# Attention's values: four heads' sums in one PSUM bank, three narrow products in place of two, and a third bank for the maxima

## The chip, the cores and the metric

The kernel runs on one core of a Trainium2 chip. The metric is device time in microseconds (us), lower is better. Before the change it is 2776.42 us, the median of three runs (2773.62 to 2778.46).

A core has five engines that run side by side, each with its own queue of instructions in a fixed order: TensorE (PE in the profile, its weight loads PEld), VectorE (DVE), ScalarE (ACT), GpSimd (POOL), and SyncE (SP), which issues the DMAs. TensorE writes its products to PSUM, where the kernel's tiles have up to 512 f32 columns on 128 partitions, each tile a bank of its own; VectorE and ScalarE read them there.

## The reference, cut to what matters

One layer of a transformer with two mixers beside each other: 2048 tokens of width 1024 and 256 context tokens. A modulated RMS norm and an input projection give the queries, keys and values of a bidirectional retention (4 heads of 128) and of an attention (8 heads of 64 in 2 groups of 4 heads, each group with one key and value head). Behind them come the output projection, a second norm, a feed-forward part of width 4096 with a squared ReLU, and a last norm. The change touches attention alone:

```python
s = jnp.einsum('bqkgd,bskd->bkgqs', q, k).astype(jnp.float32) * ATT_SCALE
p = jax.nn.softmax(s, axis=-1).astype(v.dtype)
return jnp.einsum('bkgqs,bskd->bqkgd', p, v)
```

All of it is f32: 2304 keys for each query, a softmax over them, and the weighted sum of the values.

## The kernel before, in words

The kernel has three stretches: input projections and what they need (to about 640 us), attention together with retention and the output projection (640 to 1560 us), and the feed-forward part with the last norm (from there to the end).

To keep the precision of f32 with f16 products, operands are split into a high part (the value rounded to f16) and a low part (the rest, in f16 as well). A sum of products then has three parts: high by high, low by high, and high by low.

Attention is cut into 32 groups: a block of 128 queries (`t`) and a key and value head (`g`) with its four query heads. The class `Group` (L147 to L261) holds the steps of one group. For a group:

- `piece` (L167) forms scores of 128 queries with 512 keys, with the high parts of the queries alone, in a PSUM bank with the tag `mp` (L172; L176 for the last 256 keys of two heads at once). `maximum` (L178) reduces each to its largest value with VectorE (L185). There are 18 pieces. `least` (L187) joins them into the tile `mt` (L191), `turn` (L193) transposes `mt` with TensorE into one more bank of the tag `mp` (L196), and `rows` (L198, ScalarE, L199) and `rows2` (L201, VectorE, L203) read it there, to add the negative maximum as rows to the queries `qr`.
- `scores` (L205) forms, for a tile of 128 keys, the scores of the four heads with two products of 512 columns (L209, L210) in a bank with the tag `st`. `exp` (L212, L215) writes the exponentials with ScalarE to `p`, `cast` (L217, L219) their high parts `phi`, and `low` (L221) their low parts `plo`, on GpSimd for two key tiles at once (L226) or on VectorE for one (L228).
- `values` (L230) multiplies them with the values. The tile `wv` holds for each key the 64 high parts of the value, a column of ones (so that the sum of the exponentials comes out as a 65th column), and the 64 low parts: 129 columns. For each of two key tiles and four heads there are two products: `plo` with the first 65 columns (L242), and `phi` with all 129 (L243). The sum for high times low thus has 64 columns of its own. Two heads take 258 columns, so the four heads take two banks, `o0` and `o1`. Each bank is begun, over all its columns, with a product of a tile of zeros (L234, `start=True`), and all others add to that (`start=False`).
- `evacuate` (L245) copies both banks to `so` with ScalarE (L247, L248), `invert` (L250) takes the reciprocal of the 65th column with VectorE, and `combine` (L254) adds the two sums with GpSimd (L260) and multiplies them with the reciprocal (L261).

The pools of PSUM in this stretch are `psS` (two banks each for `mp` and `st`), `psV` (one for each of `o0` and `o1`) and `psX` (two banks for retention and the output projection): eight in all. A tile of a tag takes a free place of that tag, and its first writer waits until the readers of the tile that was there are done.

The order of all instructions is set by the program: a counter `k` runs over steps, 18 for a group, and every step calls the functions that were registered for it, in the order of the phases begin, scores, piece, maximum, early, exp, cast, low, chain, pe, values, late, dma. `attention` (L1290) registers a group's 18 pieces in steps k to k + 17, each maximum one step later, `least` in step k + 18, `turn` in step k + 19 ahead of that step's piece, `rows` in k + 20 and `rows2` in k + 21. So the first pieces of a group stand around the turn of the group before it. A group's scores follow 22 steps after its first piece, and every second step holds a burst of `values`, 288 bursts in all (9 in each of 32 groups). Each engine works off its instructions in this order. The group 0 takes its maxima earlier, beside the projections.

Of the kernel before, what the change touches and what calls it, by code (L numbers as in the profile page):

```python
# [11 lines left out]
F32 = mybir.dt.float32  # L12
F32R = mybir.dt.float32r
F16 = mybir.dt.float16
BF16 = mybir.dt.bfloat16
I32 = mybir.dt.int32
AF = mybir.ActivationFunctionType
ALU = mybir.AluOpType
# [4 lines left out]
P = 128  # L23
# [6 lines left out]
NK = NT + NC  # L30
H = 4
CH = 128
HD = 64
# [4 lines left out]
EARLY = 1  # L38

ROW = 8192.0  # L40
VW = 2 * HD + 1
POOL_PAIRS = (0, 2, 4, 6, 7)

C_RQ, C_RK, C_RV, C_RG, C_AQ, C_AKV = 0, 512, 1024, 1536, 2048, 2560
# [6 lines left out]
def bc(ap, shape):  # L51
    return ap.to_broadcast(shape)
# [3 lines left out]
def layer_kernel(ctx: ExitStack, tc: tile.TileContext, a: dict, out: bass.AP):  # L56
    nc = tc.nc
    mm = nc.tensor.matmul
# [75 lines left out]
    kp = keep.enter_context(tc.tile_pool(name="kp", bufs=1, reuse_waits="tile"))  # L134
# [2 lines left out]
    ks = kp.tile([P, 2, NK * P], F16, name="ks")  # L137


    wv = kp.tile([P, 2, NK, VW + 1], F16, name="wv")  # L140
    inv = kp.tile([P, 1], F32, name="inv")

    dT, tf, tb = (kp.tile([P, 4, P], F32, name=n) for n in ("dT", "tf", "tb"))
# [3 lines left out]
    class Group:  # L147
# [16 lines left out]
            tag = f"nm{self.n}" if self.n < EARLY else "nm"  # L164
            self.nm = pool.tile([P, 2, 2, 5], F32, name="nm", tag=tag)

        def piece(self, i, pool=None, tag="mp"):  # L167
            m = self.m[i] = (pool or psS).tile([P, 512], F32, name="mp", tag=tag)
            h, r = i // 9 * 2, i % 9
            if r < 8:  # L170
                k = ks[:, self.g, r % 4 * 512 : (r % 4 + 1) * 512]
                mm(m, self.qr[:, 0, h + r // 4], k, start=True, stop=True)  # L172
            else:
                for e in range(2):
                    k = ks[:, self.g, 2048:]
                    mm(m[:, 256 * e : 256 * e + 256], self.qr[:, 0, h + e], k, start=True, stop=True)  # L176
# [14 lines left out]
                nc.vector.tensor_reduce(mt[:, :, c], nm, axis=AX.X, op=ALU.min)  # L191

        def turn(self):  # L193
            self.m = psS.tile([P, 4, P], F32, name="mp", tag="mp")
            for h in range(4):
                nc.tensor.transpose(self.m[:, h], self.mt[:, h], ident)  # L196

# [31 lines left out]

        def values(self, j):  # L230
            if j == 0:
                self.o = [psV.tile([P, 2, VW], F32, name=f"o{b}", tag=f"o{b}") for b in range(2)]
                for o in self.o:
                    mm(o, zeros, wv[:, 0, :2, :VW], start=True, stop=False)  # L234
            hi, lo = self.hi.pop(j), self.lo.pop(j)
            for i in range(2):
                v = wv[:, self.g, 2 * j + i]
                for h in range(4):
                    o = self.o[h // 2][:, h % 2]
                    c = slice(h * P, (h + 1) * P)  # L240
                    last = 2 * j + i == NK - 1 and h % 2 == 1
                    mm(o[:, : HD + 1], lo[:, i, c], v[:, : HD + 1], start=False, stop=False)  # L242
                    mm(o, hi[:, i, c], v[:, :VW], start=False, stop=last)  # L243

        def evacuate(self):  # L245
            self.so = op.tile([P, 4, VW], F32, name="so", tag="so")
            nc.scalar.activation(self.so[:, :2], self.o[0], AF.Copy)  # L247
            nc.scalar.activation(self.so[:, 2:], self.o[1], AF.Copy)  # L248

        def invert(self):  # L250
            self.r = sm.tile([P, 4], F32, name="r", tag="r")
# [2 lines left out]
        def combine(self, ats):  # L254

            if self.g == 0:
                ats[self.t] = room_tile("ma")
            at = ats[self.t][:, 4 * HD * self.g : 4 * HD * (self.g + 1)]
            at = at.rearrange("p (h d) -> p h d", h=4)
            nc.gpsimd.tensor_tensor(at, self.so[:, :, :HD], self.so[:, :, HD + 1 :], op=ALU.add)  # L260
            nc.gpsimd.tensor_tensor(at, at, bc(self.r.unsqueeze(2), [P, 4, HD]), op=ALU.mult)  # L261

    order = [(t, g) for t in range(NT - 1, -1, -1) for g in range(2)]
    groups = [Group(n, *o) for n, o in enumerate(order)]
# [2 lines left out]
    with ExitStack() as st:  # L267
# [5 lines left out]
        op = st.enter_context(tc.tile_pool(name="op", bufs=2, reuse_waits="tile"))  # L273
# [20 lines left out]
        def at(q, step, fn, *args):  # L294
            plan.setdefault((q, step), []).append((fn, args))
# [466 lines left out]
        def value_parts(q0):  # L762

            x = {}

            def load():
                nc.vector.memset(wv[:, :, :, HD : HD + 1], 1.0)
                for i in range(3):
                    x[i] = xp.tile([P, 2, 6, HD], F32, name="vn", tag="x")
                    nc.sync.dma_start(x[i], av_d[:, :, 6 * i : 6 * i + 6])  # L770
                w = xp.tile([P, P + 8], F32, name="vma", tag="x")
                x["m"], x["r"], x["s"], x["e"] = w[:, :P], w[:, P : P + 4], w[:, P + 4 : P + 5], w[:, P + 5 : P + 6]

            def greatest(i):
                v = x[i].rearrange("p g k d -> p (g k d)")
                nc.vector.tensor_reduce(
                    x["r"][:, i : i + 1], v, axis=AX.X, op=ALU.max, apply_absolute_value=True
                )
                if i == 2:
                    nc.vector.tensor_reduce(x["r"][:, 3:], x["r"][:, :3], axis=AX.X, op=ALU.max)  # L780

            def write():
                nc.sync.dma_start(vm_d, x["r"][:, 3:])

            def read():
                nc.sync.dma_start(x["m"], vm_d.partition_broadcast(P))

            def scale():
                e = x["e"]
                nc.vector.tensor_reduce(e, x["m"], axis=AX.X, op=ALU.max)  # L790
                nc.vector.tensor_scalar_max(e, e, 1e-30)
                nc.vector.tensor_single_scalar(e.bitcast(I32), e.bitcast(I32), 0x7F800000, op=ALU.bitwise_and)
                nc.vector.reciprocal(x["s"], e)
                nc.vector.tensor_scalar_mul(x["s"], x["s"], 8192.0)
                nc.vector.tensor_scalar_mul(inv, e, 2.0**-13)

            def parts(i):
                w, v = wv[:, :, 6 * i : 6 * i + 6], x[i]
                nc.vector.tensor_scalar_mul(v, v, x["s"])
                nc.scalar.activation(w[:, :, :, :HD], v, AF.Copy)  # L800
                nc.vector.tensor_tensor(w[:, :, :, HD + 1 : VW], v, w[:, :, :, :HD], op=ALU.subtract)

            at(q0, "dma", load)
            for i in range(3):
                at(q0 + 3 + i, "extra", greatest, i)
                at(q0 + 11 + i, "extra", parts, i)
            at(q0 + 5, "store", write)
            at(q0 + 7, "store", read)
            at(q0 + 10, "extra", scale)
# [340 lines left out]
        first = weights[0]  # L1150
# [74 lines left out]
    op = pool(attn, "op2", 2)  # L1225
    qp = pool(attn, "qp")
    vp = pool(attn, "vp")
    psS = pool(attn, "psS", 2, space=PSUM)
    psV = pool(attn, "psV", space=PSUM)
# [9 lines left out]
    nc.vector.tensor_tensor(unit, ident[:, 64:65], ident[:, 96:97], op=ALU.add)  # L1239
    nc.vector.tensor_tensor(unit, unit, ident[:, 80:81], op=ALU.add)  # L1240
    nc.vector.tensor_scalar_mul(unit, unit, ROW)
    zeros = vp.tile([P, P], F16, name="zeros")
    nc.vector.memset(zeros, 0.0)
    mts = [vp.tile([P, 4, P], F32, name=f"mt{i}") for i in range(2)]
    for mt in mts:
        nc.gpsimd.memset(mt, 0.0)
# [13 lines left out]
    def on(k, phase, fn, *args):  # L1260
        events.setdefault((k, phase), []).append((fn, args))
# [28 lines left out]
    def attention():  # L1290
        for n, g in enumerate(groups):
            k = NK * n
            if n > 0:
                on(k - 14 if n >= EARLY else k + NK - 6, "dma", g.load)
            else:
                on(k + NK, "begin", g.load)
            if n >= EARLY:
                on(k - 1, "late", g.minima, sm)
                for i in range(NK):
                    on(k + i, "piece", g.piece, i)  # L1300
                    on(k + i + 1, "maximum", g.maximum, i)
            on(k + NK, "chain", g.least, mts[n % 2])
            on(k + NK + 1, "piece", g.turn)
            on(k + NK + 2, "cast", g.rows)
            on(k + NK + 3, "early", g.rows2)
            k += LAG
            for i in range(NK):
                on(k + i, "scores", g.scores, i)
                on(k + i + 1, "exp", g.exp, i)
            for j in range(NK // 2):  # L1310
                on(k + 2 * j + 3, "cast", g.cast, j)
                if j in POOL_PAIRS:
                    on(k + 2 * j + 4, "low", g.low, j)
                else:
                    for i in range(2):
                        on(k + 2 * j + 4 + i, "low", g.low, j, i)
                on(k + 2 * j + 6, "values", g.values, j)
            k += NK + 5
            on(k, "cast", g.evacuate)
            on(k + 1, "chain", g.invert)  # L1320
            on(k + 2, "late", g.combine, ats)
        return NK * len(groups) + LAG + 8
# [311 lines left out]
    for n, t in enumerate(range(NT - 1, -1, -1)):  # L1634
        made_at, last = output_tile(t, R0 + 43 + RF * n, n == NT - 1)
# [362 lines left out]
    with tc.manual_schedule():  # L1998
# [8 lines left out]
        for b in range(2 * NB):  # L2007
            g = 7 * b
# [51 lines left out]
        g = NU * NS  # L2060
# [15 lines left out]
        for lo, g0 in ((0, g + 10), (4, g + 14)):  # L2076
# [3 lines left out]
            for m in range(lo, lo + 4):  # L2080
                k = g0 + 1 + m % 4 // 2
# [3 lines left out]
        g = NU * (2 * NS - 1)  # L2085
# [5 lines left out]
        for g in range(4, NU * 2 * NS):  # L2091
            b, n = divmod(g, 7)
# [26 lines left out]
        lo, hi = slice(0, HALF), slice(HALF, D)  # L2119
# [91 lines left out]
```

## Time and profile before

| | |
|---|---|
| time, median of three runs | 2776.42 us (2773.62 to 2778.46) |
| the profiled execution: its span, from the first to the last instruction (what lies around it isn't given) | 2774.9 us |
| TensorE's mean granted clock | 0.989 of full speed |
| MATMULs and LDWEIGHTS in it | 16896 each |
| products of `values` | 2304 of 65 columns, 2304 of 129 columns, 64 of zeros |

The profile is of one execution. The busy time of an engine is the time in which one of its instructions runs. Matmuls are pipelined: the next one starts while the one before is still on its way through the array, so that a row's length (0.38 us for 512 columns) is longer than the distance to the next start (0.22 us), and what a product costs a busy TensorE is the latter. Idle time in front of an instruction stands in brackets or behind the bar, with what ended it. Weight loads (LDWEIGHTS, PEld) run beside the products.

### The profile page before, as it was taken

The numbers are of one execution on the slowest core, as the hardware profiler recorded it, in microseconds if no ns is written. First come the engines' busy times: TensorE is split into PE (matmuls) and PEld (weight loads), VectorE is DVE, ScalarE is ACT, GpSimd is POOL, SyncE is SP. The second block draws the span as 40 slices with busy tenths as digits, with TensorE's granted clock in tenths as the row PEclk, the third lists the DMA queues.
The fourth block names the chain that finished last, engine by engine and source line by source line (L and its number), as shares of the span: only waits on it lengthen the run. The fifth ranks groups of instructions, "written<-read, shape, count | busy, mean of one in ns | idle before, by whom it ended". The sixth has DMA issues, their size and how long they took to land.

```text
span 2774.9 us, 45229 instructions
## 1 busy us (share of the span) xinstructions
PE 2657.9 (96%) x16896; PEld 1432.6 (52%) x16896; DVE 2103.3 (76%) x3306; ACT 1600.3 (58%) x2736; POOL 1423.2 (51%) x1182
## 2 busy tenths in 40 slices
PE   7999999888999999999999889999999999999998
PEld 2545654445666666666666544444444444444443
DVE  5857677668877777777777577989999956666676
ACT  3633762227877777787778576555554564434442
POOL 2623772365755657676667644454556721111155
PEclk9999999999999999999999999999999999999999
DMA  7478758584111231322222665665657332222223
GB/s 265 132 251 294 225 167 271 150 265 169 48 60 53 67 96 57 98 79 86 86 76 83 239 209 175 204 190 179 200 187 273 129 108 83 84 89 79 84 76 137
DMA packets 275045, 402.51 MB, mean 145 GB/s; under 512 B 107717, under 2 KB 163141, under 8 KB 272522
## 3 DMA queue, kind: packets, MB, share of 16 engines
q1 hardware_dynamic: 271802, 394.90, 43.9%
q10 hardware_dynamic: 3024, 4.72, 0.5%
q8 instruction: 133, 2.18, 0.3%
q14 instruction: 86, 0.70, 0.1%
HBM read 294.54 MB, written 105.00 MB: 144 GB/s over the span
## 4 chain that ended last, share of the span: by engine, by line
PE 76%; DVE 11%; DMA 4%; issue 3%; ACT 3%; POOL 2%; SPq 0%; POOLq 0%; ACTq 0%; DVEq 0%
PE pd L1894 6%; PE pd L1892 6%; PE pd L1893 6%; PE pu L1715 6%; PE pu L1717 6%; PE pu L1716 6%; PE pso L650 5%; PE pso L651 5%; PE pso L652 5%; PE o L243 3%; PE st L209 3%; PE st L210 3%; PE mp L172 3%; DVE plo L228 2%; DVE nm L185 2%
## 5 line engine op out<-in xcount | busy, mean ns | idle before, releaser
L185 DVE TENSOR_REDUCE nm<-mp 128x1 f32<-128x512 f32 (+1 forms) x576 | 390.3, 685 | 158.6 <-PE mp L172 131.4
L215 ACT ACTIVATE p<-st 128x512 f32<-128x512 f32 x576 | 339.1, 599 | 178.1 <-PE st L210 122.5
L226 POOL TENSOR_TENSOR plo<-p,phi 128x1024 f16<-128x1024 f32 x160 | 351.4, 2197 | 173.2 <-ACT phi L219 141.7
L1715 PE MATMUL pu<-hf,w1f 128*128 128x512 f16 x896 | 341.0, 381 | 7.2 <-ACT w L1732 3.8
L1717 PE MATMUL pu<-hf,w1f 128*128 128x512 f16 x896 | 341.0, 381 | 0.0
L1716 PE MATMUL pu<-hf,w1f 128*128 128x512 f16 x896 | 340.7, 380 | 0.0
L219 ACT ACTIVATE phi<-p 128x1024 f16<-128x1024 f32 x288 | 304.1, 1056 | 0.0
L651 PE MATMUL pso<-wlo,h 128*128 128x512 f16 (+1 forms) x816 | 296.2, 363 | 2.0 <-DVE wlo L548 2.0
L650 PE MATMUL pso<-whi,h 128*128 128x512 f16 (+1 forms) x816 | 296.5, 363 | 1.3 <-ACT whi L547 1.3
L652 PE MATMUL pso<-whi,h 128*128 128x512 f16 (+1 forms) x816 | 296.0, 363 | 0.0
L228 DVE TENSOR_TENSOR plo<-p,phi 128x512 f16<-128x512 f32 x256 | 235.1, 919 | 16.1 <-ACT phi L219 14.9
L242 PE MATMUL o<-wv,plo 128*128 128x65 f16 x2304 | 234.9, 193 | 13.0 <-POOL plo L226 6.6
L243 PE MATMUL o<-wv,phi 128*128 128x129 f16 x2304 | 242.7, 220 | 0.0
L242 PEld LDWEIGHTS <-plo 128*128 128x128 f16 x2304 | 206.1, 98 | 55.6 <-POOL plo L226 15.9
L1918 DVE SCALAR_TENSOR_TENSOR acc<-pd,scv,acc 128x512 f32<-128x512 f32 x248 | 183.1, 743 | 54.0 <-PE pd L1894 51.4
L209 PE MATMUL st<-qr,ks 128*128 128x512 f16 x576 | 219.6, 381 | 4.4 <-ACT p L215 3.8
L210 PE MATMUL st<-qr,ks 128*128 128x512 f16 x576 | 219.7, 381 | 0.1
L243 PEld LDWEIGHTS <-phi 128*128 128x128 f16 x2304 | 205.2, 97 | 21.3 <-issue 0.5
L172 PE MATMUL mp<-ks,qr 128*128 128x512 f16 x512 | 196.1, 383 | 17.2 <-DVE nm L185 17.0
L1680 POOL TENSOR_TENSOR w1s<-w1r 128x512 f32<-128x512 f32 x64 | 92.4, 1444 | 233.4 <-ACT w L1754 159.9
L1892 PE MATMUL pd<-w2t,us 128*128 128x512 f16 x496 | 188.0, 379 | 1.7 <-DVE acc L1918 1.7
L1893 PE MATMUL pd<-w2t,us 128*128 128x512 f16 x496 | 188.0, 379 | 0.0
(377 smaller groups left out, 6109.2 us busy)
## 6 DMA issues: line engine op xcount, KB each, us to landing
w2t<-w2f SPq DMA_DIRECT2D x98, 512.0 KB, 4.2
wm<-in_w_ff SPq DMA_DIRECT2D x64, 512.0 KB, 5.0
w1r<-in_w_ff SPq DMA_DIRECT2D x64, 512.0 KB, 4.7
w2f<-w2f SPq DMA_DIRECT2D x98, 256.0 KB, 2.4
wmr<-in_w_mod SPq DMA_DIRECT2D x32, 512.0 KB, 5.3
w2r<-in_w_ff SPq DMA_DIRECT2D x32, 512.0 KB, 4.2
hf<-hp SPq DMA_DIRECT2D x56, 256.0 KB, 3.5
hf<-hf SPq DMA_DIRECT2D x14, 1024.0 KB, 7.2
```

What stands on the lines that cost most here:

```text
L185: nc.vector.tensor_reduce(dst, src, axis=AX.X, op=ALU.max, negate=True)
L226: nc.gpsimd.tensor_tensor(lo, p, hi, op=ALU.subtract)
L242: mm(o[:, : HD + 1], lo[:, i, c], v[:, : HD + 1], start=False, stop=False)
L243: mm(o, hi[:, i, c], v[:, :VW], start=False, stop=last)
L650: mm(self.ps[:, c], hi[:, k], wh, start=k == 0, stop=False)
L651: mm(self.ps[:, c], hi[:, k], wl, start=False, stop=False)
L652: mm(self.ps[:, c], lo[:, k], wh, start=False, stop=k == KT - 1)
L1715: mm(pu[c], whi, hi, start=first and k == 0, stop=False, **more)
L1716: mm(pu[c], whi, lo, start=False, stop=False, **more)
L1717: mm(pu[c], wlo, hi, start=False, stop=k == 3, **more)
L1892: mm(ps, uh, wh, start=first and j == 0, stop=False, **more)
L1893: mm(ps, uh, wl, start=False, stop=False, **more)
```

## The change

- The four heads' sums take one bank: 65 columns for each head, 260 in all. The product of high and low parts is added in the first 64 of these columns, not in columns of its own. For each key tile and head there are now three products: `plo` with the 65 columns, `phi` with the 64 low parts of the values, `phi` with the 65 columns. The first product of a group begins the bank (`start=True`, for the 65 columns of the first head), and all others, the other heads' first ones too, are given as additions (`start=False`). The products of zeros and the tile of zeros go.
- `evacuate` copies one bank of 260 columns; `combine` has no sum to form any more.
- `wv` keeps its 130 columns, with the low parts from column 66 on (before from 65 on).
- The bank that comes free goes to the tag `mp`, which has three places now.

```diff
-VW = 2 * HD + 1
+VL = HD + 2
...
-    wv = kp.tile([P, 2, NK, VW + 1], F16, name="wv")
+    wv = kp.tile([P, 2, NK, VL + HD], F16, name="wv")
...
-        def piece(self, i, pool=None, tag="mp"):
-            m = self.m[i] = (pool or psS).tile([P, 512], F32, name="mp", tag=tag)
+        def piece(self, i, pool=None, tag="mp", bufs=2):
+            m = self.m[i] = (pool or psS).tile([P, 512], F32, name="mp", tag=tag, bufs=bufs)
...
-            self.m = psS.tile([P, 4, P], F32, name="mp", tag="mp")
+            self.m = psS.tile([P, 4, P], F32, name="mp", tag="mp", bufs=3)
...
         def values(self, j):
             if j == 0:
-                self.o = [psV.tile([P, 2, VW], F32, name=f"o{b}", tag=f"o{b}") for b in range(2)]
-                for o in self.o:
-                    mm(o, zeros, wv[:, 0, :2, :VW], start=True, stop=False)
+                self.o = psV.tile([P, 4, HD + 1], F32, name="o", tag="o")
             hi, lo = self.hi.pop(j), self.lo.pop(j)
             for i in range(2):
                 v = wv[:, self.g, 2 * j + i]
                 for h in range(4):
-                    o = self.o[h // 2][:, h % 2]
+                    o = self.o[:, h]
                     c = slice(h * P, (h + 1) * P)
-                    last = 2 * j + i == NK - 1 and h % 2 == 1
-                    mm(o[:, : HD + 1], lo[:, i, c], v[:, : HD + 1], start=False, stop=False)
-                    mm(o, hi[:, i, c], v[:, :VW], start=False, stop=last)
+                    first = j == i == h == 0
+                    last = 2 * j + i == NK - 1
+                    more = {"skip_group_check": h > 0}
+                    mm(o, lo[:, i, c], v[:, : HD + 1], start=first, stop=False, **more)
+                    mm(o[:, :HD], hi[:, i, c], v[:, VL:], start=False, stop=False, **more)
+                    mm(o, hi[:, i, c], v[:, : HD + 1], start=False, stop=last, **more)
 
         def evacuate(self):
-            self.so = op.tile([P, 4, VW], F32, name="so", tag="so")
-            nc.scalar.activation(self.so[:, :2], self.o[0], AF.Copy)
-            nc.scalar.activation(self.so[:, 2:], self.o[1], AF.Copy)
+            self.so = op.tile([P, 4, HD + 1], F32, name="so", tag="so")
+            nc.scalar.activation(self.so, self.o, AF.Copy)
...
-            nc.gpsimd.tensor_tensor(at, self.so[:, :, :HD], self.so[:, :, HD + 1 :], op=ALU.add)
-            nc.gpsimd.tensor_tensor(at, at, bc(self.r.unsqueeze(2), [P, 4, HD]), op=ALU.mult)
+            nc.gpsimd.tensor_tensor(at, self.so[:, :, :HD], bc(self.r.unsqueeze(2), [P, 4, HD]), op=ALU.mult)
...
-                nc.vector.tensor_tensor(w[:, :, :, HD + 1 : VW], v, w[:, :, :, :HD], op=ALU.subtract)
+                nc.vector.tensor_tensor(w[:, :, :, VL:], v, w[:, :, :, :HD], op=ALU.subtract)
...
-    zeros = vp.tile([P, P], F16, name="zeros")
-    nc.vector.memset(zeros, 0.0)
...
-                    on(k + i, "piece", g.piece, i)
+                    on(k + i, "piece", g.piece, i, psS, "mp", 3)
```

The instructions that stay stand in the same sequence on every engine; lines behind L234 have smaller numbers in the changed kernel, by one to three. The order shows the change at two places on TensorE, with the line, the operation, the tiles (out<-in), the shape and the engines for which an instruction waits. The first is the beginning of a group's first burst of `values`, before:

```order
L1507 LDWEIGHTS rl
L1507 MATMUL bank_16434<-wo,rl 128x512
L234 LDWEIGHTS zeros
L234 MATMUL o_16438<-wv,zeros 128x258 [waits Activation_49]
L234 LDWEIGHTS zeros
L234 MATMUL o_16439<-wv,zeros 128x258 [waits Activation_49]
L242 LDWEIGHTS plo [waits Pool_49]
L242 MATMUL o_16438<-wv,plo 128x65
L243 LDWEIGHTS phi
L243 MATMUL o_16438<-wv,phi 128x129
```

and now:

```order
L1504 LDWEIGHTS rl
L1504 MATMUL bank_17907<-wo,rl 128x512
L242 LDWEIGHTS plo [waits Pool_49]
L242 MATMUL o<-wv,plo 128x65 [waits Activation_49]
L243 LDWEIGHTS phi
L243 MATMUL o<-wv,phi 128x64
L244 LDWEIGHTS phi
L244 MATMUL o<-wv,phi 128x65
```

The two products of zeros are gone, their wait for ScalarE's copy of the group before is the first narrow product's, and `phi` is loaded twice for a head, once for 64 columns and once for 65.

The second place is the turn of a group's maxima (L196), with the first pieces of the next group (L172) around it; `ks` are keys, `qr` queries. Before:

```order
L210 MATMUL st<-qr,ks_6842 128x512
L196 MATMUL mp<-ident,mt_6849 128x128 [waits DVE_49,PE_49]
L196 MATMUL mp<-ident,mt_6849 128x128 x3
L172 LDWEIGHTS qr
L172 MATMUL mp<-ks,qr 128x512 [waits DVE_49]
L209 LDWEIGHTS ks
L209 MATMUL st<-qr,ks 128x512 [waits Activation_49]
L210 LDWEIGHTS ks_6842
L210 MATMUL st<-qr,ks_6842 128x512
L172 LDWEIGHTS qr
L172 MATMUL mp<-ks,qr 128x512 [waits DVE_49]
```

and now:

```order
L210 MATMUL st<-qr,ks_6842 128x512
L196 MATMUL mp<-ident,mt_6847 128x128 [waits DVE_49]
L196 MATMUL mp<-ident,mt_6847 128x128 x3
L172 LDWEIGHTS qr
L172 MATMUL mp<-ks,qr 128x512 [waits PE_49]
L209 LDWEIGHTS ks
L209 MATMUL st<-qr,ks 128x512 [waits Activation_49]
L210 LDWEIGHTS ks_6842
L210 MATMUL st<-qr,ks_6842 128x512
L172 LDWEIGHTS qr
L172 MATMUL mp<-ks,qr 128x512 [waits DVE_49]
```

No row has moved. The first piece behind the turn has lost its wait for VectorE; the second one still waits for VectorE, for an earlier maximum than before.

## The prediction

> **What bounds the kernel now.** I read the page's first part first, then the chain that ended last.
>
> ```profile
> span 2774.9 us, 45229 instructions
> PE 2657.9 (96%) x16896; PEld 1432.6 (52%) x16896; DVE 2103.3 (76%) x3306; ACT 1600.3 (58%) x2736; POOL 1423.2 (51%) x1182
> ```
>
> ```profile
> PE 76%; DVE 11%; DMA 4%; issue 3%; ACT 3%; POOL 2%; SPq 0%; POOLq 0%; ACTq 0%; DVEq 0%
> ```
>
> TensorE (PE) carries three quarters of the chain; the other engines have room on average and count only where TensorE waits for them. The change touches attention alone, so I asked for the table by stretches for 640 to 1560 us, which holds all of it, and for TensorE's own waits there (who waited for whom: us in total, times, longest us).
>
> ```profile
> 640.00:1560.00 920.00, 878.33 (x8252) 581.55 (x8252) 718.13 (x1250) 708.75 (x1156) 616.86 (x464) 0.99 0.26 81
> ```
>
> ```profile
> PE mp L172 <- DVE nm L185: 15.6, 23, 2.6
> PE o L242 <- POOL plo L226: 6.6, 10, 1.7
> PE o L242 <- DVE plo L228: 6.1, 10, 1.2
> PE st L209 <- ACT p L215: 3.8, 9, 0.9
> ```
>
> In these 920 us TensorE is busy for 878.3. So every column it no longer streams and every wait it no longer has shortens the run, as long as no other wait takes its place; VectorE's 718 us, 78%, leave it time to catch up. The largest wait is the product for the maxima (L172), which waits until VectorE has taken the maximum (L185) out of a bank. That wait and the values' products (L234, L242, L243) are what the change is about. The timeline shows where such a wait arises; first TensorE, then VectorE over the same stretch (start us, length us, engine, line).
>
> ```profile
> 1248.52 0.60 PE L196 MATMUL mp<-ident,mt 128*128 128x128 f32 x4
> 1248.95 0.38 PE L172 MATMUL mp<-ks,qr 128*128 128x512 f16 x1
> 1249.17 0.38 PE L209 MATMUL st<-qr,ks 128*128 128x512 f16 x1
> 1249.39 0.38 PE L210 MATMUL st<-qr,ks 128*128 128x512 f16 x1
> 1251.32 0.38 PE L172 MATMUL mp<-ks,qr 128*128 128x512 f16 x1 [1.55 <-DVE nm L185]
> ```
>
> ```profile
> 1247.96 0.68 DVE L185 TENSOR_REDUCE nm<-mp 128x1 f32<-128x512 f32 x1
> ...
> 1249.16 1.51 DVE L228 TENSOR_TENSOR plo<-p,phi 128x512 f16<-128x512 f32 x1
> 1250.59 0.68 DVE L185 TENSOR_REDUCE nm<-mp 128x1 f32<-128x512 f32 x1
> ...
> 1252.45 0.70 DVE L203 SCALAR_TENSOR_TENSOR qr<-mp,qr 32x512 f16<-32x512 f32 x1
> ```
>
> The turned maxima (L196) sit in one of the two mp banks until their last reader (L203) ends at 1253.15. Until then a single bank turns round, and each piece waits for the maximum of the piece just before it: the piece at 1251.32 starts when the maximum that began at 1250.59 ends, and that one had stood behind 1.51 us of VectorE's other work.
>
> **The change part by part.** Four groups of rows, of the whole run, give counts and lengths (count | busy us, mean ns).
>
> ```profile
> L242 PE MATMUL o<-wv,plo 128*128 128x65 f16 x2304 | 234.9, 193 | 13.0 <-POOL plo L226 6.6 <-DVE plo L228 6.1
> L243 PE MATMUL o<-wv,phi 128*128 128x129 f16 x2304 | 242.7, 220 | 0.0
> L234 PE MATMUL o<-wv,zeros 128*128 128x258 f16 x64 | 12.3, 274 | 0.0
> L247 ACT ACTIVATE so<-o 128x258 f32<-128x258 f32 x32 | 12.3, 386 | 17.9 <-PE o L243 17.3
> L248 ACT ACTIVATE so<-o 128x258 f32<-128x258 f32 x32 | 12.3, 384 | 0.0
> L260 POOL TENSOR_TENSOR ma<-so 128x256 f32<-128x256 f32 x32 | 24.8, 774 | 10.4 <-ACT so L248 10.4
> ```
>
> *Products of zeros.* What a product costs a busy TensorE is the distance to the next start, not its length.
>
> ```profile
> 1003.70 0.38 PE L234 MATMUL o<-wv,zeros 128*128 128x258 f16 x2
> 1003.92 0.19 PE L242 MATMUL o<-wv,plo 128*128 128x65 f16 x1
> ```
>
> Two take 0.22 us, one 0.11 us; 64 of them are 7.0 us. All of it stands on TensorE's own path, so it goes: -7 us. The wait for ScalarE's evacuation of the last group, which L234 carried, passes to the first L242, with the whole burst queued behind it as before; it ends earlier, since one copy of 260 columns stands where two of 258 stood.
>
> *Values' products.* The columns stay: 65 + 129 before, 65 + 64 + 65 after, 194 each. What is new is a third product and a third weight load per head and key tile, 2304 of each. One burst before, eight pairs:
>
> ```profile
> 1000.41 0.19 PE L242 MATMUL o<-wv,plo 128*128 128x65 f16 x1
> 1000.44 0.22 PE L243 MATMUL o<-wv,phi 128*128 128x129 f16 x1
> 1000.50 0.19 PE L242 MATMUL o<-wv,plo 128*128 128x65 f16 x1
> 1000.53 0.22 PE L243 MATMUL o<-wv,phi 128*128 128x129 f16 x1
> ...
> 1001.06 0.22 PE L243 MATMUL o<-wv,phi 128*128 128x129 f16 x1
> 1001.11 0.38 PE L209 MATMUL st<-qr,ks 128*128 128x512 f16 x1
> ```
>
> The burst takes 0.70 us, 0.0875 for a pair. The mean lengths give the price of a column: (220 - 193) / 64 = 0.42 ns, so that the wide product takes 0.027 us more than the narrow one, and the narrow one is (0.0875 - 0.027) / 2 = 0.030 us, as the rows have it (0.41 to 0.44, 0.50 to 0.53). With 24 narrow products the new burst is 24 x 0.030 = 0.72 us: +0.02 us in each of 288 bursts (2304 / 8), +6 us. The rows are given to a hundredth; a burst of 0.71 makes it 0.031 for a product, 0.744 for a burst and +13 us, the upper end of this reading. The lower end is 0, since the columns are the same; a gain is excluded, since no column goes.
>
> Does the weight load fit into 0.03 us? The loads of the same burst:
>
> ```profile
> 1000.41 0.10 PEld L243 LDWEIGHTS <-phi 128*128 128x128 f16 x1
> 1000.44 0.10 PEld L242 LDWEIGHTS <-plo 128*128 128x128 f16 x1
> ```
>
> The load for L243 starts with the product at 1000.41, and its own product starts at 1000.44. So a load can be ready after 0.03 us, its recorded 0.10 us notwithstanding. But this trace shows it for one narrow product at a time, always followed by a wide one in which the next load has 0.06 us. The longest value for a narrow product that I found stands right behind a stall:
>
> ```profile
> 703.29 0.20 PE L242 MATMUL o<-wv,plo 128*128 128x65 f16 x1 [0.90 <-POOL plo L226]
> 703.33 0.22 PE L243 MATMUL o<-wv,phi 128*128 128x129 f16 x1
> ```
>
> That is 0.04 us. I take 0.030, the value of the unstalled rows, and keep 0.04 for a rival. The Trainium skill speaks against me here: TensorE: Matmul & The Clock Gate, Weight-path perf modes, gives about 40 ns per matmul for a stream with small free dimension and fast weight load (measured there with fp8). By that figure a burst would be 0.96 us and the sum +75 us instead of +6; the single pairs of this trace, at 0.03 us, are faster than it, and no run here shows a stream of nothing but narrow ones. The same page's Back-to-back issue gap has about 81 ns per pair of load and matmul at 128 columns; there the trace differs, with 0.05 to 0.06 us at 129.
>
> *Third bank.* At stake are the 15.6 us of 23 waits. The view counts idle time from a product's modelled end, 0.38 us after its start, while the next could start after 0.22 (1249.17 and 1249.39), so each wait costs 0.16 us more: 15.6 + 23 x 0.16 = 19.3 us. At the place shown all 1.71 us (1249.61 to 1251.32) would go: with a third bank the piece needs the maximum before, which ended at 1248.64. Not every wait goes whole. A TensorE that is ahead meets the lo parts (L226, L228), for which it already waits 12.7 us in 20 places, and neither VectorE nor GpSimd makes them sooner because a bank is free. I take 70%, an estimate between these: -13.5 us. The ends are -19.3 and -4. A loss is excluded by the order: on each engine the remaining instructions stand in the same sequence, so an earlier start delays nobody, save for shared memory ports, a microsecond or two.
>
> *ScalarE and GpSimd.* 64 copies become 32 of nearly the same length (-12.3 us of ScalarE), and L260 goes (-24.8 us of GpSimd). Both engines wait for TensorE far more than it for them; I take 0, at most the 3.8 us that L209 waits for ScalarE.
>
> *Sum:* -7 + 6 - 13.5 = -14.5 us, on the span of 2774.9: 2760.4. The median of the runs lies 1.5 us above this span, so 2762. Its own ends: best -7 + 0 - 19.3 - 3.8, 2746; worst of the same mechanism -7 + 13 - 4, 2778.
>
> **The rivals.**
>
> *A: the wait only moves* (TensorE, no longer held by the bank, runs into L226 and L228). For it: 20 waits of that kind already, and the lo parts stand in the same queues as before. Against it: VectorE idles a fifth of the 920 us, and a wait for its lo part is 0.6 us long on average, so its lateness is not a backlog that lasts. If a third or less of the bank's gain stays, the sum lies between -7 + 6 - 4.5 and -7 + 13 - 0: 2771 to 2782.
>
> *B: the weight load paces the burst.* Three loads and three products in place of two, none of them with a wide product to hide behind. At 0.04 us per product the burst is 24 x 0.04 = 0.96, +0.26 x 288 = +75 us; with the other terms +54: about 2830. It decides from (0.70 + 20.5 / 288) / 24 = 0.032 us per product on, where the other two terms are used up. For it: the 0.04 at 703.29, and that load and product start together, so that a load can't begin before the product ahead has begun. Against it: 0.03 in row after row, where that load had no wide product to hide behind either, since it ran beside a narrow one. The page's 40 ns would give this time.
>
> *C: the bank isn't free when it should be*, because the pool hands the third place to another tile than the waiting piece, and the change does only what the products do: -7 + 6 = -1, 2775. Against it stands the order itself, where the piece behind the turn has lost its wait for VectorE.
>
> **How the numbers follow.** A measurement of this kernel can tell about 0.2%, 5.6 us, from no change. Forecast: 0.66, with 0.05 more beyond its best end. A and C: 0.17. B: 0.09, and 0.03 for products between 0.031 and 0.04 us. So faster 0.71, same 0.17, slower 0.12. The range from 2747 to 2778, the forecast's own ends, leaves out what lies beyond the best end (0.05), B with what leads to it (0.12) and the upper part of A (0.03), two in ten. The predicted time is that of the forecast, 2762.
>
> **What would show it.** Right: L234 gone; bursts of 24 products from 0.71 to 0.75 us; the wait of L172 for L185 under 5 us; the waits of L242 for L226 and L228 up by a few us at most; attention shorter by 10 to 20 us and the feed-forward part unchanged. Wrong: bursts of 0.8 us and more (B); L242's waits up by about what L172's lost (A); L172 waiting as before (C).

## The result, and the profile after

The changed kernel takes 2764.64 us (median; 2761.49 to 2765.97, 4 runs) against 2777.06 us before (2773.62 to 2778.46, 4 runs): ratio 0.9955, 95% interval 0.9942 to 0.9969, 12 us faster. The prediction was 2762 us, 2747 to 2778. The sum held; two of its terms did not, as the experiments show. The profiled execution took 2761.49 us, its span is 2759.7.

The page's first part and the chain that ended last, of the changed kernel:

```profile
span 2759.7 us, 49635 instructions
PE 2651.4 (96%) x19136; PEld 1436.3 (52%) x19136; DVE 2099.9 (76%) x3305; ACT 1590.9 (58%) x2704; POOL 1399.1 (51%) x1150
```

```profile
PE 79%; DVE 9%; ACT 4%; issue 3%; DMA 3%; POOL 2%; SPq 0%; POOLq 0%; DVEq 0%; ACTq 0%
```

TensorE has 2240 products more (2304 third products, less 64 of zeros), ScalarE 32 copies less, GpSimd 32 operations less, and TensorE's share of the chain has grown. How long attention takes is read from its first and last L209, a line that has the same number in all kernels here (first and last start stand behind the lengths). First before, then after:

```profile
L209 PE MATMUL st<-qr,ks x576: 376/379/634, 641.3 to 1550.6; 128*128 128x512 f16 x192
```

```profile
L209 PE MATMUL st<-qr,ks x576: 376/379/634, 640.1 to 1535.6; 128*128 128x512 f16 x192
```

909.3 us became 895.5: 13.8 us less, of the 15.2 by which the span is shorter. The stretch ahead of it, which the change doesn't touch, varies by four us among the kernels here (the first L209 starts between 637.6 and 641.9 us); so the stretch from first to last L209 is the finer measure of what a change in attention does, and it is used below beside the times. It is one execution for each kernel.

The stretch has an error of its own. In spells of 3.4 us or a few times that, TensorE's granted clock is at half, in every profile here; one of them, as the table by stretches shows it for the kernel before (the third number from the end is the clock):

```profile
1342.90:1346.30 3.40, 3.01 (x21) 1.91 (x21) 1.72 (x3) 1.37 (x2) 1.90 (x1) 0.50 0.93 287
```

In such a spell products of 512 columns start 0.427 us apart, otherwise 0.216, so that 3.4 us of it cost up to 1.7 us. Half of the spells' length in the stretch is 6.0 us before and 1.9 us after. So up to 4.1 of the 13.8 us come from where the spells fell, and between 9.7 and 13.8 us are the change's, which agrees with the 12 us of the times (9 to 16 by their interval).

One burst of `values` after, from its first product to the next L209:

```profile
1259.82 0.19 PE L242 MATMUL o<-wv,plo 128*128 128x65 f16 x1
1259.85 0.20 PE L243 MATMUL o<-wv,phi 128*128 128x64 f16 x1
1259.88 0.19 PE L244 MATMUL o<-wv,phi 128*128 128x65 f16 x1
1259.91 0.19 PE L242 MATMUL o<-wv,plo 128*128 128x65 f16 x1
...
1260.53 0.19 PE L244 MATMUL o<-wv,phi 128*128 128x65 f16 x1
1260.56 0.38 PE L209 MATMUL st<-qr,ks 128*128 128x512 f16 x1
```

24 products in 0.74 us, 0.03 us for each. Over all 288 bursts the median is 0.732 us, before 0.699 without the zeros: 288 x 0.033 = 9.5 us, about +10. So a weight load fits into 0.03 us 24 times in a row: 0.732 / 24 is 30.5 ns. The Trainium skill (TensorE: Matmul & The Clock Gate, Weight-path perf modes) has about 40 ns per matmul with a small free dimension, measured with fp8; this trace, with f16, is faster than that.

The place that the prediction showed, a turn and the pieces behind it, now:

```profile
1241.98 0.60 PE L196 MATMUL mp<-ident,mt 128*128 128x128 f32 x4
1242.42 0.38 PE L172 MATMUL mp<-ks,qr 128*128 128x512 f16 x1
1242.63 0.38 PE L209 MATMUL st<-qr,ks 128*128 128x512 f16 x1
1242.85 0.38 PE L210 MATMUL st<-qr,ks 128*128 128x512 f16 x1
1243.07 0.38 PE L172 MATMUL mp<-ks,qr 128*128 128x512 f16 x1
```

The last row had 1.55 us of idle time in front of it and has none. TensorE's waits in attention (640 to 1560 us) after the change:

```profile
PE o L242 <- DVE plo L228: 11.2, 12, 2.0
PE o L242 <- POOL plo L226: 6.9, 13, 1.2
...
PE st L209 <- ACT p L215: 3.1, 7, 0.8
PE mp L196 <- DVE mt L191: 2.5, 5, 0.6
PE st L209 <- DMA qr<-aq: 2.0, 1, 2.0
```

L172's 15.6 us are gone altogether, and L242's waits for its lo parts have grown from 12.7 to 18.1 us.

### The profile page after: what moved, and what is told of

Read it like the earlier page. It is cut to its first block, busy times and chain, and to the rows that moved or that the text cites. A ratio compares the mean times of both kernels' runs of the same rounds, so it can differ in the third digit from the quotient of the medians.

```text
span 2759.7 us, 49635 instructions
## 1 busy us (share of the span) xinstructions
PE 2651.4 (96%) x19136; PEld 1436.3 (52%) x19136; DVE 2099.9 (76%) x3305; ACT 1590.9 (58%) x2704; POOL 1399.1 (51%) x1150
## 4 chain that ended last, share of the span: by engine, by line
PE 79%; DVE 9%; ACT 4%; issue 3%; DMA 3%; POOL 2%; SPq 0%; POOLq 0%; DVEq 0%; ACTq 0%
PE pu L1712 6%; PE pu L1713 6%; PE pu L1714 6%; PE pd L1891 6%; PE pd L1889 6%; PE pd L1890 6%; PE pso L649 5%; PE pso L650 5%; PE pso L651 5%; PE st L210 3%; PE st L209 3%; PE mp L172 3%; DVE plo L228 2%; PE o L242 2%; PE o L243 2%
## 5 line engine op out<-in xcount | busy, mean ns | idle before, releaser
L226 POOL TENSOR_TENSOR plo<-p,phi 128x1024 f16<-128x1024 f32 x160 | 353.3, 2209 | 168.1 <-ACT phi L219 112.8
L219 ACT ACTIVATE phi<-p 128x1024 f16<-128x1024 f32 x288 | 303.3, 1053 | 0.0
L242 PE MATMUL o<-wv,plo 128*128 128x65 f16 x2304 | 241.7, 193 | 18.6 <-DVE plo L228 11.2
L243 PE MATMUL o<-wv,phi 128*128 128x64 f16 x2304 | 241.7, 194 | 0.0
L228 DVE TENSOR_TENSOR plo<-p,phi 128x512 f16<-128x512 f32 x256 | 232.0, 907 | 12.0 <-ACT phi L219 10.0
L244 PE MATMUL o<-wv,phi 128*128 128x65 f16 x2304 | 240.6, 192 | 0.0
L242 PEld LDWEIGHTS <-plo 128*128 128x128 f16 x2304 | 212.8, 96 | 53.3 <-POOL plo L226 16.8
L209 PE MATMUL st<-qr,ks 128*128 128x512 f16 x576 | 218.6, 380 | 5.7 <-ACT p L215 3.1
L243 PEld LDWEIGHTS <-phi 128*128 128x128 f16 x2304 | 212.1, 97 | 22.9
L244 PEld LDWEIGHTS <-phi 128*128 128x128 f16 x2304 | 212.6, 99 | 0.0
L172 PE MATMUL mp<-ks,qr 128*128 128x512 f16 x512 | 195.5, 382 | 0.4 <-DVE nm L185 0.4
```

The source lines that it names most:

```text
L226: nc.gpsimd.tensor_tensor(lo, p, hi, op=ALU.subtract)
L242: mm(o, lo[:, i, c], v[:, : HD + 1], start=first, stop=False, **more)
L243: mm(o[:, :HD], hi[:, i, c], v[:, VL:], start=False, stop=False, **more)
L244: mm(o, hi[:, i, c], v[:, : HD + 1], start=False, stop=last, **more)
```

## The experiments

Ratios are to the kernel before, run on the same chip in the same session; the changed kernel has 0.9955. A hundredth of a per cent is 0.28 us.

**The terms one by one.** My theory was the prediction's sum with the measured burst: zeros -7, third product +9, third bank -13.5, ScalarE and GpSimd nothing. The rival was that the relief of ScalarE and GpSimd brings the gain.

*e1_two_banks.* The changed kernel; the freed bank stays unused:

```diff
-            self.m = psS.tile([P, 4, P], F32, name="mp", tag="mp", bufs=3)
+            self.m = psS.tile([P, 4, P], F32, name="mp", tag="mp", bufs=2)
...
-                    on(k + i, "piece", g.piece, i, psS, "mp", 3)
+                    on(k + i, "piece", g.piece, i, psS, "mp", 2)
```

> The changed kernel, but with two places for mp again; the freed bank stays unused. Theory (the third bank brings the gain): only -7 us for the zeros and +9 us for the bursts (288 x (0.73 - 0.70)) are left, so 2777 + 2 = 2779 us, and the wait of L172 for L185 is back at about 16 us. Rival (the gain comes from the relief of ScalarE and GpSimd, 12 and 25 us less busy, or from the zeros): it stays near the changed kernel, 2764 to 2770 us, though L172 waits again.

2767.42 us, ratio 0.9972 (0.9962 to 0.9981). TensorE's waits:

```profile
PE mp L172 <- DVE nm L185: 13.5, 19, 2.6
PE o L242 <- POOL plo L226: 5.5, 10, 1.2
PE o L242 <- DVE plo L228: 4.1, 7, 1.3
PE st L209 <- ACT p L215: 2.8, 6, 0.8
```

L172 waits again, as both said, but the time is 7.8 us below before instead of 2 above. The theory falls here: something else than the bank brings about 10 us.

*e2_no_zeros.* The kernel before without the products of zeros:

```diff
-                for o in self.o:
-                    mm(o, zeros, wv[:, 0, :2, :VW], start=True, stop=False)
...
-                    mm(o[:, : HD + 1], lo[:, i, c], v[:, : HD + 1], start=False, stop=False)
-                    mm(o, hi[:, i, c], v[:, :VW], start=False, stop=last)
+                    more = {"skip_group_check": h % 2 > 0}
+                    if j == i == 0:
+                        mm(o, hi[:, i, c], v[:, :VW], start=h % 2 == 0, stop=False, **more)
+                    mm(o[:, : HD + 1], lo[:, i, c], v[:, : HD + 1], start=False, stop=False, **more)
+                    if j or i:
+                        mm(o, hi[:, i, c], v[:, :VW], start=False, stop=last, **more)
```

> The kernel before, without the products of zeros: in each bank the first wide product of the first key tile begins the sums, the other head's first wide product is an addition; nothing else is changed. Theory: 64 x 0.11 us on TensorE's path, -7 us, 2770 us. Rival (TensorE runs into the next wait for a lo part, so that the time moves there): 0 to -2 us, with the wait of L242 up by 5 us or more.

2767.06 us, ratio 0.998 (0.9971 to 0.9989): -5.5 us; the attention stretch (639.2 to 1543.1) is 5.4 us shorter than before. L242's place (here L243) waits 13.8 us in place of 12.7. The theory holds: the interval (3.1 to 8.0 us) has the 7 us in it and leaves out the rival's 0 to 2. Whether a part of the 7 us is given back it can't tell.

*e3_split.* The kernel before, the wide product in two:

```diff
-                    mm(o, hi[:, i, c], v[:, :VW], start=False, stop=last)
+                    mm(o[:, HD + 1 :], hi[:, i, c], v[:, HD + 1 : VW], start=False, stop=False)
+                    mm(o[:, : HD + 1], hi[:, i, c], v[:, : HD + 1], start=False, stop=last)
```

> The kernel before, with the wide product split in two, 64 and 65 columns, each in the columns it had; two banks, zeros and two places for mp as before. Theory (what the third product costs is the product, whichever columns it adds to): bursts 0.73 us, +9 us, 2786 us. Rival (what costs is adding into the same columns as the product just before): bursts 0.71 us or less, +3 us or less.

2781.26 us, ratio 1.0027 (1.0016 to 1.0037): +7.5 us. One burst of it:

```profile
1277.19 0.19 PE L242 MATMUL o<-wv,plo 128*128 128x65 f16 x1
...
1277.40 0.20 PE L243 MATMUL o<-wv,phi 128*128 128x64 f16 x1
1277.44 0.19 PE L244 MATMUL o<-wv,phi 128*128 128x65 f16 x1
```

The median burst is 0.738 us, though no product here adds to columns of the one before it. So the price is the product's own, and the rival falls. 288 x 0.039 = 11 us of longer bursts became 7.5 us of time (4 to 10 by the interval) and 6.5 us of the attention stretch (640.0 to 1555.8): the rest seems to have been paid out of shorter waits (L172's 14.0 us in place of 15.6, L242's 11.6 in place of 12.7).

*e4_turn_own.* The changed kernel; the third bank is the turned maxima's own:

```diff
-            self.m = psS.tile([P, 4, P], F32, name="mp", tag="mp", bufs=3)
+            self.m = psS.tile([P, 4, P], F32, name="mp", tag="tn", bufs=1)
...
-                    on(k + i, "piece", g.piece, i, psS, "mp", 3)
+                    on(k + i, "piece", g.piece, i, psS, "mp", 2)
```

> The changed kernel, with the third bank given to the turned maxima alone (a tag of its own), so that the pieces have two places at all times, in place of three shared ones. Theory (the wait arises at the turn, where one place turns round): nearly all of the gain stays, 2764 to 2767 us, L172 waiting 3 us or less. Rival (any late maximum stops TensorE, at the turn or not): a good third of the waits is back, 5 us or more of L172's, 2769 us or more.

2761.15 us, ratio 0.9961 (0.9947 to 0.9974), the same as the changed kernel.

```profile
PE o L242 <- DVE plo L228: 8.3, 11, 1.4
...
PE mp L172 <- DVE nm L185: 2.3, 4, 1.1
```

2.3 of L172's 13.5 us are back, less than the rival's 5, and the lo parts are waited for 3.5 us less than in the changed kernel. Most of the wait of L172 arises at the turn, as the prediction read it.

**The relief of ScalarE and GpSimd.** A new theory: the copies and L260 that went made ScalarE and GpSimd earlier, and that reaches TensorE. Six kernels put the work back, with results that nobody uses; on three places or two:

```diff
+            sp = op.tile([P, 4, HD + 1], F32, name="sp", tag="sp")
+            nc.scalar.activation(sp, self.o, AF.Copy)
             nc.scalar.activation(self.so, self.o, AF.Copy)
...
+            nc.gpsimd.tensor_tensor(at, self.so[:, :, :HD], self.so[:, :, 1:], op=ALU.add)
             nc.gpsimd.tensor_tensor(at, self.so[:, :, :HD], bc(self.r.unsqueeze(2), [P, 4, HD]), op=ALU.mult)
```

*e5_all_undone* (two places, both put back):

> The changed kernel with two places for mp, with a second copy of 260 columns by ScalarE at each evacuation and a second operation of 256 columns by GpSimd at each combine (both results unused): of the change only the zeros and the third product are left. Theory (the 8 us by which e1_two_banks beat its sum are the relief of ScalarE and GpSimd): they are lost again, 2774 to 2778 us, the stretch from the first to the last L209 at 909 to 912 us. Rival (longer bursts give VectorE and GpSimd time, so that part of their cost is paid by shorter waits whatever ScalarE and GpSimd do): 2767 to 2770 us, that stretch at 902 to 906 us.

2778.48 us, ratio 1.0013 (1.0005 to 1.0022). The theory holds: 11 us above e1_two_banks.

*e6_gpsimd_op* (three places, GpSimd's) and *e7_scalar_copy* (three places, ScalarE's):

> The changed kernel, with a second operation of 256 columns by GpSimd at each combine (result unused), 32 x 0.77 us as before the change. Theory (relief of GpSimd counts): 3 to 6 us more than the changed kernel, with L242's wait for L226 up by that. Rival (it is off the path): no more than 1 us.

> The changed kernel, with a second copy of 260 columns by ScalarE ahead of each evacuation (result unused), 32 x 0.39 us as before the change. Theory (relief of ScalarE counts): 2 to 5 us more than the changed kernel, with the waits of L209 for L215 and of L242 for its lo parts up. Rival (it is off the path): no more than 1 us.

2764.37 us, 0.9959 (0.9943 to 0.9974), and 2765.13 us, 0.9967 (0.9956 to 0.9979): 1 and 3 us above the changed kernel, within the intervals. By the times alone neither is told from nothing beside three places. Among TensorE's waits, L242's for L226 rose by 1.9 us in the first and L209's for ScalarE by 1.4 in the second.

*e9_three_both* (three places, both), *e10_two_gpsimd* and *e11_two_scalar* (two places, one of them):

> The changed kernel with three places for mp, and both the second copy by ScalarE and the second operation by GpSimd (results unused). Beside e5_all_undone, which has two places and both, it gives what the third bank is worth while ScalarE and GpSimd have their old work. Theory (the bank and the relief take away the same lateness, so that either does much of it alone): the bank is worth 9 to 13 us here, against about 5 beside the relieved engines: 2765 to 2769 us. Rival (they are separate terms that add): the bank is worth 5 us here too, 2771 to 2774 us.

> The changed kernel with two places for mp and the second operation by GpSimd alone (result unused). With two places, both undone cost 11 us (e5_all_undone against e1_two_banks). If GpSimd's operation is most of that, 2773 us or more, and ScalarE's kernel stays below 2771; if each has a share, 2771 to 2775 in both.

> The changed kernel with two places for mp and the second copy by ScalarE alone (result unused). If ScalarE's copy is most of the 11 us, because the exponentials and with them the lo parts and VectorE's maxima come later, 2773 us or more, and GpSimd's kernel stays below 2771; if each has a share, 2771 to 2775 in both.

2769.73 us, 0.9983 (0.9974 to 0.9992); 2773.05 us, 1.0000 (0.9991 to 1.0008); 2772.99 us, 0.9990 (0.9981 to 0.9999). Beside two places each of the two alone is told from nothing: against e1_two_banks GpSimd's costs 8 us and ScalarE's 5, with an uncertainty of 3.5 us. So each has a share. With these the eight kernels of the table are complete: two or three places for mp, with none, one or both of the old pieces of work put back. Ratio, and the attention stretch in us:

| | none | GpSimd's | ScalarE's | both |
|---|---|---|---|---|
| two places | 0.9972, 903.0 | 1.0000, 908.5 | 0.9990, 907.9 | 1.0013, 911.5 |
| three places | 0.9955, 895.5 | 0.9959, 898.6 | 0.9967, 899.8 | 0.9983, 903.5 |
| the third bank | -7.5 us | -9.9 us | -8.1 us | -8.0 us |

Half of the length of the half-clock spells in each of these stretches, and what is left of the stretch without it, in us:

| | none | GpSimd's | ScalarE's | both |
|---|---|---|---|---|
| two places | 2.8, 900.2 | 5.9, 902.6 | 4.7, 903.3 | 3.4, 908.1 |
| three places | 1.9, 893.6 | 1.7, 896.9 | 3.9, 895.9 | 5.9, 897.6 |
| the third bank | -6.6 us | -5.7 us | -7.4 us | -10.5 us |

In the stretch as it stands, the third bank is worth 7.5 to 9.9 us in all four columns, and the relief 8.5 us in the first row (911.5 - 903.0) and 8.0 in the second. Without the spells the bank is worth 5.7 to 10.5 us and the relief 7.9 and 4.0. By the ratios the bank has 5 to 11 us and the relief 11 and 8, each with an uncertainty of 3 to 5 us. So both are there, at about 8 us each, and in the first row the relief is above 3.8 us by every measure.

Whether the two terms add is not settled. Set beside both old pieces of work, the bank is worth 0.5 us more than beside none by the first table, 3.9 us more by the second, and 3.6 us more by the ratios, within their uncertainty. My theory that bank and relief do each other's work had 9 to 13 us against 5, its rival 5 and 5; the time, 2769.73 us, fell between their ranges. How the relief divides between GpSimd and ScalarE is open as well: the differences, 1 to 8 us, change with the measure.

How the relief gets to TensorE is seen in several views. ScalarE at a group's end, in the changed kernel and then in e9_three_both:

```profile
1256.74 0.39 ACT L248 ACTIVATE so<-o 128x260 f32<-128x260 f32 x1
1257.02 1.05 ACT L219 ACTIVATE phi<-p 128x1024 f16<-128x1024 f32 x1
```

```profile
1262.40 0.39 ACT L249 ACTIVATE sp<-o 128x260 f32<-128x260 f32 x1
1262.68 0.38 ACT L250 ACTIVATE so<-o 128x260 f32<-128x260 f32 x1
1262.95 1.06 ACT L219 ACTIVATE phi<-p 128x1024 f16<-128x1024 f32 x1
```

The copy stands ahead of the cast (L219), for which the lo parts wait. VectorE's wait for it, in the changed kernel and in e7_scalar_copy:

```profile
DVE plo L228 <- ACT phi L219: 10.0, 12, 3.6
```

```profile
DVE plo L228 <- ACT phi L219: 17.7, 28, 3.6
```

One copy more costs VectorE 7.7 us in 16 more waits, and VectorE's maxima and lo parts stand behind them in its queue. GpSimd's operation works in the other direction: its lo part (L226) comes later, and ScalarE, which can't write new exponentials until a place of `p` is free, waits longer; in the changed kernel and in e6_gpsimd_op:

```profile
ACT p L215 <- POOL plo L226: 11.7, 13, 1.8
```

```profile
ACT p L215 <- POOL plo L226: 16.5, 17, 1.7
```

GpSimd's operation reaches VectorE without a wait in the list, too. The rows of VectorE's lo parts in the changed kernel and in e6_gpsimd_op (count | busy us, mean ns | idle time in front):

```profile
L228 DVE TENSOR_TENSOR plo<-p,phi 128x512 f16<-128x512 f32 x256 | 232.0, 907 | 12.0 <-ACT phi L219 10.0
```

```profile
L228 DVE TENSOR_TENSOR plo<-p,phi 128x512 f16<-128x512 f32 x256 | 238.4, 932 | 12.8 <-ACT phi L219 10.9
```

Most lo parts take 0.68 us; 95 of 256 in the changed kernel, and 102 in e6_gpsimd_op, take from 0.71 to 2.5 us. Each of these ends 0.54 to 0.56 us after an instruction of GpSimd that ran beside it: VectorE is held up until GpSimd is done. The prediction's row of 1.51 us at 1249.16 is of this kind. The operation put back costs VectorE 6 us in this way.

At TensorE itself, both pieces put back raise the waits of L172, L242 and L209 together by 7.6 us beside two places (e1_two_banks to e5_all_undone: 2.4, 3.6 and 1.6) and by 3.5 us beside three (the changed kernel to e9_three_both: L242 2.0, L209 1.5). That is close to the 7.9 and 4.0 us of the second table.

**The third product's 0.03 us.** In the changed kernel's trace the start behind the 64-column product (L243 to L244) comes after 32.0 ns in the mean, the two others after 29.7 and 29.5.

*e8_by_kind:* the four heads' products of a kind stand together:

```diff
+                last = 2 * j + i == NK - 1
+                cs = [slice(h * P, (h + 1) * P) for h in range(4)]
                 for h in range(4):
-                    o = self.o[:, h]
...
                     first = j == i == h == 0
...
+                    mm(self.o[:, h], lo[:, i, cs[h]], v[:, : HD + 1], start=first, stop=False, skip_group_check=True)
+                for h in range(4):
+                    mm(self.o[:, h, :HD], hi[:, i, cs[h]], v[:, VL:], start=False, stop=False, skip_group_check=True)
+                for h in range(4):
+                    mm(self.o[:, h], hi[:, i, cs[h]], v[:, : HD + 1], start=False, stop=last, skip_group_check=True)
```

> The changed kernel, with the products of a key tile ordered by kind: the lo parts with four heads, then the high parts with the low values for four heads, then the high parts with the high values. So no product adds to the columns of the one before, no weights are loaded twice in a row, and two products of 64 columns stand side by side. In the changed kernel the product behind the 64-column one starts 32 ns after it, the others 29.5. If that is the repeated load of the same weights or the same columns: all 29.5, bursts 0.71 us, up to 5 us faster. If it is the 64 columns (the product ends before the next load is ready): the 64-column products are followed after 32 to 34 ns wherever they stand, bursts 0.73, no change.

2759.83 us, ratio 0.9947 (0.9933 to 0.996). A burst (rows of one kind are merged, four products each):

```profile
1263.01 0.28 PE L240 MATMUL o<-wv,plo 128*128 128x65 f16 x4
1263.13 0.28 PE L242 MATMUL o<-wv,phi 128*128 128x64 f16 x4
1263.25 0.28 PE L244 MATMUL o<-wv,phi 128*128 128x65 f16 x4
...
1263.72 0.38 PE L209 MATMUL st<-qr,ks 128*128 128x512 f16 x1
```

This one takes 0.71 us, the median is 0.725, 2 us less over all bursts. Between two products of 64 columns lie 29.7 ns in the mean, so the 64 columns alone aren't the cause. In e3_split, where the columns differ but the same weights are loaded twice in a row, the second of them comes after 34.0 ns. Together this points to the repeated load of the same weights, but it doesn't show it: in e8_by_kind the step from the last 64-column product to the first of 65 columns, with other weights, still takes 31.2 ns in the mean, and single steps there lie between 28 and 35 ns, which is not explained. The time is 2 us below the changed kernel's, within the intervals.

*e12_kind_turn:* e8_by_kind with e4_turn_own's bank:

> The products ordered by kind, as in e8_by_kind, and the third bank given to the turned maxima alone, as in e4_turn_own; the outputs are those of the reference. If the two small gains add (2 us of the bursts, and up to 1 us), 2758 to 2761 us; if not, the same as e8_by_kind, 2760 to 2764.

2761.27 us, ratio 0.9954 (0.9942 to 0.9967). The interval, 3.5 us to either side, reaches into the ranges of both expectations, so it isn't shown whether the small gains add. e8_by_kind, e4_turn_own, e12_kind_turn and the changed kernel can't be told apart by their intervals; none is shown to beat the changed kernel.

## Why the prediction was right, and where it wasn't

*Zeros, -7 us: right.* 5.5 us by itself in e2_no_zeros, with the 7 inside its interval.

*Values' products, +6 us, 0 to 13: in the range, a little low.* The burst came out at 0.732 us, not 0.72, +10 us. With all else undone, e5_all_undone stands at +3.6 us (+2.2 in the attention stretch), where -7 + 10 make +3. The upper end, +13 us, was worked out unevenly: it takes 0.031 us per product from an old burst of 0.71 us, but subtracts 0.70; from 0.71 it is (0.744 - 0.71) x 288 = +10.

*Rival B: refuted.* It would have decided from 0.032 us per product on; there were 0.0305.

*Third bank, "I take 70%, an estimate between these: -13.5 us": mis-sized.* The wait of L172 went whole, 13.5 us by the view between e1_two_banks and the changed kernel. But the wait of L242 for VectorE's lo parts rose from 4.1 to 11.2 us, and for GpSimd's from 5.5 to 6.9. About 8 us stayed (5 to 11 by the kernels and measures above), some 40% of the 19.3 at stake, not 70%. What the prediction named as next in line was the right place; it gave it too little weight. Its rival A, in which a third or less would stay, was close. VectorE's 22% of idle time, the reason for expecting more, did not keep its lo parts from being late.

*"I take 0, at most the 3.8 us that L209 waits for ScalarE": the step that failed.* The relief was worth about 8 us, twice the bound (4 to 11 by the kernels and measures above; beside two places 11 by the times, with an uncertainty of 3.5). The bound counted the one wait in which TensorE names ScalarE. ScalarE's and GpSimd's lateness reaches TensorE under other names as well: through the cast to VectorE's lo parts and maxima, through the places of `p` to the exponentials, and through the lo parts on VectorE that last until GpSimd is done. The two errors, 5.5 us too much for the bank and 8 too little for the relief, nearly cancel; with the products' 4 us more the sum is -7 + 10 - 8 - 8 = -13, against 12 measured. That the time came out within 3 us of the forecast is in part luck.

*The signs it named.* L234 gone, bursts of 0.73 us, no wait of L172, attention shorter by 10 to 14 us, and the rest behind the last L209 the same to 0.3 us: as forecast. L242's waits up by "a few us at most" was not: 5.4 us more than before, and 8.5 more than with two places and the rest of the change.

## What to carry to other kernels

A wait that a view lists under one engine's name is no bound for what that engine's relief is worth: an operation that stands in a queue ahead of what others wait for costs them too, here about 8 of the 37 us by which the two engines had less to do. And a bank more takes a wait away where it is listed, but the lateness that caused it stays and is met again at the next thing that TensorE needs; with VectorE busy 78% of the stretch, somewhat less than half of it was really saved. To tell such terms apart, put the removed work back with unused results, and read the stretch that the change touches beside the whole time, after a look at how much half-clock time each profile has in it: here that differed by up to 4 us.

## What the runs showed of the hardware

- Products of 64 and 65 f16 columns, each with a weight load of its own, follow one another every 30.5 ns for a burst of 24.
- Where the same weights were loaded twice in a row, the second product came after 32.0 ns (the changed kernel) and 34.0 ns (e3_split), the others after 29.5 to 29.7. That the repeated load is the cause is not shown: without it, e8_by_kind has one step of 31.2 ns.
- In spells of 3.4 us or a few times that, with a granted clock of 0.5, products of 512 columns started every 0.427 us in place of 0.216, and the narrow products of `values` every 0.054 us in place of 0.030 (the first in the kernel before, the second in e1_two_banks and e5_all_undone).
- A subtraction on VectorE (L228, 0.68 us) that ran longer ended 0.54 to 0.56 us after an instruction of GpSimd that ran beside it: 94 of 94 before, 95 of 95 in the changed kernel, 102 of 102 in e6_gpsimd_op, the longest 2.6 us. In the changed kernel 14 others began while an instruction of GpSimd had 0.18 us or more to run, and weren't held up: 12 of them beside one line, L1279, another at the same moment as GpSimd's instruction, to 0.01 us. What sets them apart is open.
